# Order of a gated pair's low part and of a weight block's high part in the second expert product

## Chip, cores and metric

The kernel runs on one core of a Trainium2 chip. Its time is the device time of one execution in microseconds; before the change the median of three runs is 1809.54 us (1803.93 to 1812.57). A profile is one further execution, recorded instruction by instruction.

## The reference

One decoder block for 512 tokens of width 1024, all in float32. A normalised input feeds a convolution module and a causal attention with a forgetting gate; both are mixed and added to the input. Then comes a feed-forward part with 16384 single-neuron experts, of which each token takes 128 (8 heads, 16 each, from a product-key search):

```
experts = (e1 * 128 + e2)              # 128 experts for each token
a   = gelu(u[experts] . h) * gates     # peer_u rows, one number per expert
out = sum over experts of a * v[expert] # peer_v rows
x   = x + out;  result = rmsnorm(x)
```

## The kernel before

The first 128 tokens (tile 0) are computed as the reference writes it: GpSimd gathers one row of `peer_u` or `peer_v` per expert slot with an indirect DMA (`fetch`, L1089), and VectorE takes a dot product with it (L1110) or adds it, scaled, to the output (L1116). There are 256 such rows, 128 of each kind, in a generator (`gathered`, L1101) that the main loops call a few rows at a time.

For the other 384 tokens the kernel computes all experts densely. The first expert product multiplies all of `peer_u`, in 128 blocks of 128 experts, with the tokens; its results after gelu are kept in `Sd` in memory, two blocks (a pair) at a time. A gate table `Gd` holds, for every expert and token, the gate or zero. The second expert product, where the change is, multiplies the results by the gates and by `peer_v`: for each of 128 blocks, a weight of 128 experts x 1024 and the gated values of 128 experts x 384 tokens, accumulated over all blocks in six PSUM tiles (L1261 to L1276).

TensorE works in a float32 format of reduced width, so every operand X is split into a high part (rounded copy, made by ScalarE) and a low part (X minus the high part, made by VectorE), and each product is three matmuls (`mm3`, L170): low of the left with high of the right, high with low, high with high. The left operand is the gated pair, `ah` and `al`; the right is the weight block, `whi` and `wlo`. A block has 3 token tiles x 2 column halves x 3 = 18 matmuls, in the order `al`x`whi` (L172), `ah`x`wlo` (L173), `ah`x`whi` (L174).

Weights come through a stream. SP's queue loads raw blocks `wraw` (three buffers), a split gives `whi` and `wlo` (four buffers of each). `next_w` (L162) hands block i to the product and calls `pump` (L135). `pump` first calls `flush` (L122), which issues the splits that are pending: `whi` on ScalarE, `wlo` on VectorE. Then it issues the next raw load, and then it only notes block i+3 as pending. So in block i's call the split of block i+2 is issued, high and low together.

`a_pair` (L1182) prepares the next pair at the start of every second block: it issues on ScalarE's queue the loads of a later `Sb` (L1179) and, every fourth pair, of a later `G` (L1171); VectorE multiplies `Sb` by `G` (L1192); then `split` (L205) issues `ah` on ScalarE (L206) and `al` on VectorE (L208), which needs `ah`. There are two buffers of `ah` and of `al`. The order in which the code issues instructions is the order on each engine; nothing reorders them.

VectorE's order in an even block is thus: the product `Sb`, `al`, one `wlo`, one or two gathered rows; in an odd block: one `wlo`, one or two rows.

Of the kernel before, what the change touches and what calls it, by code (L numbers as in the profile page):

```python
# [9 lines left out]
F32 = mybir.dt.float32  # L10
# [5 lines left out]
AF = mybir.ActivationFunctionType  # L16
ALU = mybir.AluOpType
# [70 lines left out]
def body(ctx, tc, x, xT, w_ct, w_v, w_f, w_co, w_fo, w_o, w_q, keys, pu, pv, pur, vecs, conv_w,  # L88
         bf, g2, gf, maskneg, sel, out):
    nc = tc.nc  # L90
    pool = nc.gpsimd
    dve = nc.vector
# [29 lines left out]
    def flush(hi_to=4, lo_to=4):  # L122
        q = D // 4
        for p in pend:
            eng, lo, raw, hi, nh, nl = p
            if nh < hi_to:
                nc.scalar.activation(hi[:, nh * q:hi_to * q], raw[:, nh * q:hi_to * q], AF.Copy)  # L127
                p[4] = hi_to
            if nl < lo_to:
                c = slice(nl * q, lo_to * q)  # L130
                eng.tensor_tensor(lo[:, c], raw[:, c], hi[:, c].bitcast(F32), op=ALU.subtract)  # L131
                p[5] = lo_to
        pend[:] = [p for p in pend if p[5] < 4]

    def pump(n_split, n_raw):  # L135
        flush()
        while state["raw"] < min(n_raw, len(stream)):
            i = state["raw"]
            raws[i] = base.tile([P, D], F32, tag="wraw", name="wraw", bufs=WRAW)
            if i:  # L140
                nc.sync.dma_start(raws[i], stream[i][0])
            else:
                for c in (slice(0, 512), slice(512, D)):
                    nc.sync.dma_start(raws[i][:, c], stream[i][0][:, c])
                    nc.sync.dma_start(xTt[:, c.start // 512, :], xT[c.start // 512])
            state["raw"] += 1
        while state["split"] < min(n_split, len(stream)):
            i = state["split"]
            kind = stream[i][2]
            if kind != "w":  # L150
                if kind not in dest:
                    return
                hi, lo = dest[kind].pop(0)
            else:
                hi = base.tile([P, D], F32R, tag="whi", name="whi", bufs=WSPL)
                lo = base.tile([P, D], F32R, tag="wlo", name="wlo", bufs=WSPL)
            raw = raws.pop(i)
            pend.append([stream[i][1], lo, raw, hi, 0, 0])
            parts[i] = (hi, lo)
            state["split"] += 1  # L160

    def next_w(held=0):  # L162
        i = state["used"]
        state["used"] += 1
        pump(i + WSPL - held, i + WSPL - held + WRAW - 1)
        if any(p[1] is parts[i][1] for p in pend):
            flush()
        return parts.pop(i)

    def mm3(o, l, r, first, last):  # L170
        (lh, ll), (rh, rl) = l, r
        nc.tensor.matmul(o, ll, rh, start=first, stop=False)  # L172
        nc.tensor.matmul(o, lh, rl, start=False, stop=False)  # L173
        nc.tensor.matmul(o, lh, rh, start=False, stop=last)  # L174
# [30 lines left out]
    def split(hi, lo, src, scale=None):  # L205
        nc.scalar.activation(hi, src, AF.Copy, scale=1.0 if scale is None else scale)  # L206
        if scale is None:
            dve.tensor_tensor(lo, src, hi.bitcast(F32), op=ALU.subtract)  # L208
        else:
            dve.scalar_tensor_tensor(lo, src, scale, hi.bitcast(F32), op0=ALU.mult, op1=ALU.subtract)  # L210
# [920 lines left out]
    def bgrun(us, g):  # L1131
        debt[g] = debt.get(g, 0.0) + us
        while debt[g] > 0:
            r = next(g, None)
            if r is None:
                return False
            debt[g] -= r[0]
        return True
# [3 lines left out]
    def u_block(b):  # L1142
        c, n = divmod(b, SB2)
        kept = c >= NK // SB2 - KEEP
        if n == 0:
            if kept:
                gel[c] = vp[0].tile([P, SB2, TD], F32, tag="kept", name="kept", bufs=KEEP)
            else:
                gel[c] = gl.tile([P, SB2, TD], F32, tag="gel", name="gel", bufs=2)
        p = proj(hden, False)  # L1150
        nc.scalar.activation(gel[c][:, n, :], p[:, :TD], AF.Gelu_apprx_tanh)  # L1151
        if n == SB2 - 1:
            if kept:
                Ss[c] = gel.pop(c)
            else:
                nc.sync.dma_start(Sd[c], gel.pop(c))
# [9 lines left out]
    def load_g(n):  # L1166
        if n >= NK // GB8:
            return
        g = VORD[n * GB8] // GB8
        t = vp[0].tile([P, TD // TG, GB8, TG], F32, tag="G", name="G", bufs=GLD)  # L1170
        nc.scalar.dma_start(t.rearrange("p g b t -> p g (b t)"), Gd[g])  # L1171
        Gs[g] = t

    def load_s(n):
        if n >= NK // SB2 or n < KEEP:
            return
        c = VORD[n * SB2] // SB2
        t = vp[0].tile([P, SB2, TD], F32, tag="S", name="Sb", bufs=3)
        nc.scalar.dma_start(t, Sd[c])  # L1179
        Ss[c] = t  # L1180

    def a_pair(k):  # L1182
        if k >= NK // SB2:
            return
        c = VORD[k * SB2] // SB2
        g, n = divmod(c * SB2, GB8)
        if n == 0:
            load_g(k * SB2 // GB8 + GLD - 1)
        load_s(k + 2)
        a = Ss.pop(c)  # L1190
        a4 = a.rearrange("p n (g t) -> p n g t", t=TG)
        dve.tensor_tensor(a4, a4, Gs[g][:, :, n:n + SB2, :].rearrange("p g n t -> p n g t"), op=ALU.mult)  # L1192
        hi = vp[0].tile([P, SB2, TD], F32R, tag="ah", name="ah", bufs=ABUF)
        lo = vp[0].tile([P, SB2, TD], F32R, tag="al", name="al", bufs=ABUF)
        split(hi, lo, a)
        As[k] = (hi, lo)

    def open_second():
        while bgrun(12, bgr) or later:
            while later:  # L1200
                later.pop(0)()
        gp_ctx.close()
        pd_ctx.close()
        vp.append(ctx.enter_context(tc.tile_pool(name="phe", bufs=1, side="right")))
# [3 lines left out]
    for b in range(UE + 1, NK):  # L1208
        u_block(b)
        room = U_DVE  # L1210
        if len(later) > busy:
            later.pop(0)()
            room += U_SC
        share = U_BG if ready else 0.0
        busy = bgrun(room - share, bgr)
        more = busy or later
        if ready:
            bgrun(share if more else U_END, bgg)
        if not vp and (not more or b == NK - VAHEAD):
            open_second()  # L1220
            opened = b
        if vp and b == min(opened + VWAIT, NK - KEEP * SB2 + 1):
            vready.append(1)
            for g in range(GLD - 1):
                load_g(g)
        if b == NK - KEEP * SB2 + 4:
            a_pair(0)
    gl_ctx.close()
    h2_ctx.close()

# [30 lines left out]
    for b in range(NK - SB2):  # L1261
        c, n = divmod(b, SB2)
        if n == 0:
            a_pair(c + 1)
        hi, lo = next_w()
        ah, al = As[c]
        if b == 0:
            left = 2 * NG - ngath[0]
        while 2 * NG - ngath[0] > left * (NK - 5 - b) // (NK - 4):
            if next(bgg, None) is None:  # L1270
                break
        for i in range(1, NT):
            k = slice((i - 1) * P, i * P)
            for f, d in enumerate(halves):
                mm3(oacc[i - 1][f], (ah[:, n, k], al[:, n, k]), (hi[:, d], lo[:, d]), b == 0, False)
# [89 lines left out]
```

## Time and profile before

| What | Value |
|---|---|
| Profiled execution, own time | 1810.52 us |
| Its span, first to last instruction | 1808.5 us |
| Mean granted TensorE clock | 0.997 of full speed |
| VectorE (DVE) busy | 1507.4 us |
| ScalarE (ACT) busy | 877.3 us |
| GpSimd (POOL) busy | 388.0 us |
| Bytes moved | 432.92 MB, 239 GB/s |
| Landing of a load of `Sb` / `G`, median | 6.6 us / 10.0 us |

PE is TensorE's matmuls, PEld its weight loads, SPq and ACTq DMA issues. Engines overlap, so busy times don't add up. A matmul's recorded duration includes its pipeline, so consecutive ones overlap; the distance between two starts is the pace. In the profile the second expert product is the stretch from about 1257 to 1799 us, with PE lines named `whi,al`, `wlo,ah` and `whi,ah`.

### The profile page before, as it was taken

The page shows a single profiled execution, that of the slowest core. Times are in us where ns is not written, and L with a number is a line of the kernel's source. Part 1 is how long each engine was busy: PE and PEld are TensorE (multiplying, and loading weights), DVE is VectorE, ACT ScalarE, POOL GpSimd, SP SyncE. Part 2 cuts the span into 40 slices and gives each one's busy share as a digit, 9 for nine tenths or more (in the row PEclk, how much of TensorE's full clock was granted, in tenths as well). Part 3 has the DMA queues.
Part 4 walks back from the last instruction along what each step waited for, and adds up shares of the span by engine and source line. Part 5 has one row for each costly group of instructions (what it writes and reads, how often), then busy time and mean ns, then how long its engine had stood idle before and what let it go on. Part 6 is the DMA issues. An engine that isn't in the chain of part 4 may idle for free.

```text
span 1808.5 us, 25395 instructions
## 1 busy us (share of the span) xinstructions
PE 1767.8 (98%) x9289; PEld 1538.4 (85%) x9289; DVE 1507.4 (83%) x2649; ACT 877.3 (49%) x1622; POOL 388.0 (21%) x303
## 2 busy tenths in 40 slices
PE   8999999999999999999999999999999999999997
PEld 7887777788888889999999999999787787787786
DVE  5799999998755699999888987766888888888887
ACT  5665665535524323344488499953333333333333
POOL 0000000000000000023322322143443444454440
PEclk9999999999999999999999999999999999999999
DMA  6332222122343125578989899999999999999994
GB/s 224 97 94 72 86 76 80 61 82 93 117 148 129 63 78 161 180 250 286 312 277 319 313 314 320 318 355 408 369 384 382 372 385 380 378 384 373 373 335 147
DMA packets 164477, 432.92 MB, mean 239 GB/s; under 512 B 13696, under 2 KB 63488, under 8 KB 162304
## 3 DMA queue, kind: packets, MB, share of 16 engines
q1 hardware_dynamic: 111840, 239.37, 38.5%
q0 software_dynamic: 39424, 138.43, 21.6%
q10 hardware_dynamic: 13088, 53.50, 7.8%
q8 instruction: 73, 1.20, 0.3%
q14 instruction: 52, 0.43, 0.1%
HBM read 376.20 MB, written 50.86 MB: 236 GB/s over the span
## 4 chain that ended last, share of the span: by engine, by line
PE 50%; DVE 22%; ACT 12%; DMA 10%; issue 5%; ACTq 0%; POOL 0%; SPq 0%; POOLq 0%; DVEq 0%
PE mm L172 15%; PE mm L173 15%; PE mm L174 15%; DMA wraw<-in_pv 7%; DVE wlo L131 5%; DVE x L1116 5%; DVE y L498 5%; ACT whi L127 4%; ACT ohs L1067 2%; DMA wraw<-in_pu 2%; ACT ah L206 2%; DVE Sb L1192 2%; PE pvp L1076 2%; DVE grow L1110 2%; DVE ptl L637 1%
## 5 line engine op out<-in xcount | busy, mean ns | idle before, releaser
L131 DVE TENSOR_TENSOR wlo<-wraw,whi 128x1024 fp32r<-128x1024 f32 (+1 forms) x434 | 432.8, 1005 | 101.3 <-ACT whi L127 97.1
L127 ACT ACTIVATE whi<-wraw 128x1024 fp32r<-128x1024 f32 (+1 forms) x429 | 373.7, 893 | 94.6 <-DMA wraw<-in_pv 38.8
L172 PE MATMUL mm<-h2h,wlo 128*128 128x384 f32 (+1 forms) x1152 | 397.8, 345 | 2.1 <-DVE wlo L131 1.6
L173 PE MATMUL mm<-h2l,whi 128*128 128x384 f32 (+1 forms) x1152 | 392.8, 341 | 0.5 <-DVE h2l L208 0.5
L174 PE MATMUL mm<-h2h,whi 128*128 128x384 f32 (+1 forms) x1152 | 393.0, 341 | 0.0
L1097 POOL DMA_INDIRECT grow<-in_pur,sx x128 | 179.1, 1399 | 613.8 <-DVE grow L1110 369.1
L1097 POOL DMA_INDIRECT grow<-in_pv,sx x128 | 185.9, 1452 | 230.1 <-DVE x L1116 203.4
L172 PEld LDWEIGHTS mm<-h2h,wlo 128*128 128x128 f32 x1152 | 216.8, 188 | 7.6 <-DVE wlo L131 2.0
L173 PEld LDWEIGHTS mm<-h2l,whi 128*128 128x128 f32 x1152 | 217.1, 188 | 5.7 <-DVE h2l L208 1.1
L174 PEld LDWEIGHTS mm<-h2h,whi 128*128 128x128 f32 x1152 | 216.8, 188 | 5.3
L173 PE MATMUL mm<-wlo,ah 128*128 128x512 f32 x512 | 203.4, 397 | 9.4 <-DVE wlo L131 9.0
L172 PE MATMUL mm<-whi,al 128*128 128x512 f32 x512 | 199.9, 390 | 0.2 <-DVE al L208 0.2
L174 PE MATMUL mm<-whi,ah 128*128 128x512 f32 x512 | 199.7, 390 | 0.0
L206 ACT ACTIVATE ah<-Sb 128x768 fp32r<-128x768 f32 x60 | 50.8, 846 | 303.9 <-DVE Sb L1192 254.5
L498 DVE SCALAR_TENSOR_TENSOR y<-z,cw,y 128x512 f32<-128x512 f32 x240 | 174.2, 749 | 1.1 <-ACT y L495 0.2
L1116 DVE SCALAR_TENSOR_TENSOR x<-grow,dots,x 128x1024 f32<-128x1024 f32 x128 | 164.5, 1285 | 1.1
L172 PE MATMUL mm<-hTh,wlo 128*128 128x512 f32 x384 | 161.3, 420 | 3.2 <-DVE qa L570 1.7
L1110 DVE SCALAR_TENSOR_TENSOR grow<-grow,hd 128x1024 f32<-128x1024 f32 x128 | 155.0, 1217 | 0.7 <-DMA grow<-in_pur,sx 0.7
L174 PE MATMUL mm<-hTh,whi 128*128 128x512 f32 x384 | 150.6, 392 | 0.0
L173 PE MATMUL mm<-hTl,whi 128*128 128x512 f32 x384 | 150.0, 391 | 0.0
L1151 ACT ACTIVATE gel<-mm 128x384 f32<-128x384 f32 x118 | 57.7, 489 | 182.4 <-PE mm L174 110.1
L173 PEld LDWEIGHTS mm<-wlo,ah 128*128 128x128 f32 x512 | 96.0, 188 | 41.9 <-DVE wlo L131 23.0
(284 smaller groups left out, 2943.9 us busy)
## 6 DMA issues: line engine op xcount, KB each, us to landing
wraw<-in_pu SPq DMA_DIRECT2D x128, 512.0 KB, 4.9
wraw<-in_pv SPq DMA_DIRECT2D x128, 512.0 KB, 6.4
wraw<-in_w_ct SPq DMA_DIRECT2D x48, 512.0 KB, 3.5
Gd<-gst SPq DMA_DIRECT2D x24, 1024.0 KB, 9.8
G<-Gd ACTq DMA_DIRECT2D x16, 1536.0 KB, 10.0
Sb<-Sd ACTq DMA_DIRECT2D x60, 384.0 KB, 6.6
Sd<-gel SPq DMA_DIRECT2D x59, 384.0 KB, 6.1
wraw<-in_w_q SPq DMA_DIRECT2D x16, 512.0 KB, 3.5
```

Source lines behind the costliest of these rows:

```text
L127: nc.scalar.activation(hi[:, nh * q:hi_to * q], raw[:, nh * q:hi_to * q], AF.Copy)
L131: eng.tensor_tensor(lo[:, c], raw[:, c], hi[:, c].bitcast(F32), op=ALU.subtract)
L172: nc.tensor.matmul(o, ll, rh, start=first, stop=False)
L173: nc.tensor.matmul(o, lh, rl, start=False, stop=False)
L174: nc.tensor.matmul(o, lh, rh, start=False, stop=last)
L206: nc.scalar.activation(hi, src, AF.Copy, scale=1.0 if scale is None else scale)
L498: dve.scalar_tensor_tensor(acc, z[:, w:w + S], cw[:, j, w:w + 1], acc, op0=ALU.mult, op1=ALU.add)
L1067: nc.scalar.activation(o[:, 3, g, :, t], o[:, 1, g, :, t], AF.Copy, scale=gl32[:, t0 + u:t0 + u + 1])
L1097: pool.indirect_dma_start(out=t, out_offset=None, in_=src, in_offset=bass.IndirectOffsetOnAxis(ap=sx[:, n % NG:n % NG + 1], axis=0))
L1110: yield 1.25, dve.scalar_tensor_tensor(t, t, 1.0, hd, op0=ALU.mult, op1=ALU.mult, accum_out=dots[:, k:k + 1])
L1116: yield 1.28, dve.scalar_tensor_tensor(o, t, dots[:, k:k + 1], o, op0=ALU.mult, op1=ALU.add)
L1151: nc.scalar.activation(gel[c][:, n, :], p[:, :TD], AF.Gelu_apprx_tanh)
```

## The change

`a_pair` no longer issues `al` itself. It issues `ah` and puts the subtraction on a list `apend`; `a_low` issues what is on the list. In the first product's loop (first pair) `a_low` follows `a_pair` at once; in the second product it is called behind the block's gathered rows. And each block of the second product calls `flush(4, 0)` behind `next_w`: it issues the whole high part of whatever is pending (block i+3) and none of its low part, which stays pending until the next block's `flush`.

```
         hi = vp[0].tile([P, SB2, TD], F32R, tag="ah", name="ah", bufs=ABUF)
         lo = vp[0].tile([P, SB2, TD], F32R, tag="al", name="al", bufs=ABUF)
-        split(hi, lo, a)
+        nc.scalar.activation(hi, a, AF.Copy)
         As[k] = (hi, lo)
+        apend.append(lambda: dve.tensor_tensor(lo, a, hi.bitcast(F32), op=ALU.subtract))
+
+    apend = []
+
+    def a_low():
+        while apend:
+            apend.pop(0)()
...
         if b == NK - KEEP * SB2 + 4:
             a_pair(0)
+            a_low()
...
         if n == 0:
             a_pair(c + 1)
         hi, lo = next_w()
+        flush(4, 0)
         ah, al = As[c]
         if b == 0:
             left = 2 * NG - ngath[0]
         while 2 * NG - ngath[0] > left * (NK - 5 - b) // (NK - 4):
             if next(bgg, None) is None:
                 break
+        a_low()
         for i in range(1, NT):
```

## Rows read from the trace of the kernel before

**Rows 1.** The page, part 1: busy us, share of the span, instructions.
```profile
PE 1767.8 (98%) x9289; PEld 1538.4 (85%) x9289; DVE 1507.4 (83%) x2649; ACT 877.3 (49%) x1622; POOL 388.0 (21%) x303
```

**Rows 2.** The page, part 4: chain that ended last, shares by engine.
```profile
PE 50%; DVE 22%; ACT 12%; DMA 10%; issue 5%; ACTq 0%; POOL 0%; SPq 0%; POOLq 0%; DVEq 0%
```

**Rows 3.** Second product: us, PE, PEld, DVE, ACT, POOL busy, clock, DMA share, GB/s.
```profile
1257.00:1799.00 542.00, 532.41 (x2306) 429.20 (x2304) 468.82 (x469) 180.82 (x204) 230.66 (x161) 1.00 0.95 359
```

**Rows 4.** Waits, 1257 to 1799 us: us in total, times, longest us.
```profile
DVE al L208 <- ACT ah L206: 61.1, 63, 1.2
...
ACT whi L127 <- DMA wraw<-in_pv: 35.9, 17, 4.3
...
PEld mm L173 <- DVE wlo L131: 23.0, 40, 1.0
...
DVE wlo L131 <- ACT whi L127: 8.3, 9, 1.8
```

**Rows 5.** Timeline of VectorE, two pairs: start us, us, instruction [idle before <-releaser].
```profile
1434.05 0.96 DVE L208 TENSOR_TENSOR al<-Sb,ah 128x768 fp32r<-128x768 f32 x1 [1.24 <-ACT ah L206]
...
1441.58 0.96 DVE L208 TENSOR_TENSOR al<-Sb,ah 128x768 fp32r<-128x768 f32 x1 [0.96 <-ACT ah L206]
1442.53 1.23 DVE L131 TENSOR_TENSOR wlo<-wraw,whi 128x1024 fp32r<-128x1024 f32 x1
1443.67 2.60 DVE L1116 SCALAR_TENSOR_TENSOR x<-grow,dots,x 128x1024 f32<-128x1024 f32 x2
...
1448.57 0.95 DVE L1192 TENSOR_TENSOR Sb<-Sb,G 128x768 f32<-128x768 f32 x1
1450.47 0.96 DVE L208 TENSOR_TENSOR al<-Sb,ah 128x768 fp32r<-128x768 f32 x1 [0.96 <-ACT ah L206]
```

**Rows 6.** Timeline of TensorE: first and last start, two blocks, first and last stalls.
```profile
1257.05 0.39 PE L172 MATMUL mm<-whi,al 128*128 128x512 f32 x1
...
1273.84 0.50 PE L173 MATMUL mm<-wlo,ah 128*128 128x512 f32 x1
...
1405.01 0.39 PE L172 MATMUL mm<-whi,al 128*128 128x512 f32 x1
...
1409.09 0.39 PE L172 MATMUL mm<-whi,al 128*128 128x512 f32 x1
...
1409.89 0.50 PE L173 MATMUL mm<-wlo,ah 128*128 128x512 f32 x1 [0.42 <-DVE wlo L131]
...
1766.70 0.39 PE L174 MATMUL mm<-whi,ah 128*128 128x512 f32 x1
...
1798.74 0.39 PE L174 MATMUL tp<-whi,ah 128*128 128x512 f32 x1
```

**Rows 7.** Timelines of VectorE and TensorE at the start of the second product.
```profile
1261.07 0.96 DVE L1192 TENSOR_TENSOR kept<-kept,G 128x768 f32<-128x768 f32 x1
...
1263.94 1.22 DVE L131 TENSOR_TENSOR wlo<-wraw,whi 128x1024 fp32r<-128x1024 f32 x1
...
1265.26 0.39 PE L172 MATMUL mm<-whi,al 128*128 128x512 f32 x1
...
1267.38 1.22 DVE L131 TENSOR_TENSOR wlo<-wraw,whi 128x1024 fp32r<-128x1024 f32 x1
```

**Rows 8.** Raw blocks: landing in the stretch; a late load and its two `wlo`.
```profile
DMA to landing us min/median/max: 3.4/6.3/11.3
...
1281.17 1.23 DVE L131 TENSOR_TENSOR wlo<-wraw,whi 128x1024 fp32r<-128x1024 f32 x1
...
1282.42 10.44 DMA wraw<-in_pv
...
1294.04 1.22 DVE L131 TENSOR_TENSOR wlo<-wraw,whi 128x1024 fp32r<-128x1024 f32 x1 [1.83 <-ACT whi L127]
```

**Rows 9.** DMA totals: first 1300 to 1700 us, then 1220.7 to 1266.
```profile
DMA packets 39654, 151.05 MB, mean 378 GB/s; under 512 B 4396, under 2 KB 4396, under 8 KB 38097
...
DMA packets 4481, 18.51 MB, mean 409 GB/s; under 512 B 509, under 2 KB 509, under 8 KB 4175
```

More of the change, by code (lines that the diff above doesn't have):

```diff
@@ L1194, in a_pair, with a_low @@
         lo = vp[0].tile([P, SB2, TD], F32R, tag="al", name="al", bufs=ABUF)
-        split(hi, lo, a)
+        nc.scalar.activation(hi, a, AF.Copy)
         As[k] = (hi, lo)
+        apend.append(lambda: dve.tensor_tensor(lo, a, hi.bitcast(F32), op=ALU.subtract))
+    apend = []
+    def a_low():
+        while apend:
+            apend.pop(0)()
     def open_second():
@@ L1227, in body @@
             a_pair(0)
+            a_low()
     gl_ctx.close()
@@ L1265, in body @@
         hi, lo = next_w()
+        flush(4, 0)
         ah, al = As[c]
@@ L1271, in body @@
                 break
+        a_low()
         for i in range(1, NT):
```

## Prediction

> **What bounds the kernel now.** I read the page's busy times first: TensorE is busy for 98% of the span [rows 1], which by itself leaves nothing to gain. The chain of waits tells otherwise: half of it is TensorE and 22% VectorE [rows 2]. The change touches only the second expert product, so everything below is read in its stretch, 1257 to 1799 us, where VectorE is busy for 468.8 of 542 us [rows 3].
>
> The waits of that stretch [rows 4] name who holds whom. VectorE waits 61.1 us, 63 times, for ScalarE's `ah` before it can form `al`, and 8.3 us for `whi`. TensorE's weight loader waits for `wlo` 40 times. VectorE's busy time and its two waits add up to 538.2 of 542 us: it has no free time in the stretch, though it is busy for only 86% of it.
>
> The timeline shows how. A pair of blocks with three gathered rows takes VectorE 8.89 us from one `al` to the next (1441.58 to 1450.47), a pair with two takes 7.53 us (1434.05 to 1441.58); in both, 0.96 us pass idle between the end of the `Sb` product and `al`, which is ScalarE making `ah` [rows 5]. TensorE needs 4.08 us for an undisturbed block (1405.01 to 1409.09), so 8.16 for a pair [rows 6]. So VectorE falls behind by 0.73 us in a three-row pair and gains 0.63 in a two-row one. The price is in [rows 6]: at 1409.89 a matmul on `wlo` starts 0.80 us after the one before it, where the pace is 4.08/18 = 0.227, because that `wlo` had just been finished.
>
> I went through the starts of all 2304 matmuls of the stretch. A step that is more than 0.1 us over the pace occurs 55 times, first at 1273.84 and last at 1766.70 (a late `wlo` also stretches the step behind it) [rows 6]; the excess sums to 17.2 us. Checked from outside: first start 1257.05, last 1798.74, so about 541.9 us for 128 blocks; 128 x 4.08 = 522.2. Of the 19.7 us between, 17.2 are these stalls and 2.5 are small irregularities that the change does not address. 17.2 us is what there is to win; the 61 us of `al` waits is not, since TensorE becomes the bound long before.
>
> **The change part by part.** No instruction is added or removed: the same `ah`, `al`, `whi`, `wlo`, and the same transfers on SP, ScalarE and GpSimd queues. Two orders change.
>
> First, `al`. It moves from directly behind ScalarE's `ah` to behind the next `wlo` and the block's gathered rows. The 0.96 us in which `ah` is made is now covered by that `wlo`, whose successor starts 1.14 us later (1442.53 to 1443.67), and by at least one row of 1.28 us [rows 5]. That takes 0.96 us out of VectorE's pair: 8.89 becomes 7.93 and 7.53 becomes 6.57, against 8.16 of TensorE. So even the three-row pair now gains 0.23 us of lead on TensorE, the other 1.59. VectorE's total need falls to 468.8 + 8.3 = 477 us, below 522: the bound moves to TensorE. If that cover were gone (the `wlo` not ready to run), the wait only moves, and nothing is saved.
>
> Second, the high part `whi` of the newest weight block. It is issued at the end of a block's `next_w`, no longer at the start of the following one: 125 of 128 `whi`, all behind `ah` on ScalarE. This is what makes the first part work: the next block's `wlo` now finds `whi` done, where it used to stand behind `ah` on ScalarE. ScalarE is busy for 181 of 542 us [rows 3], so its time is free. The cost: a ScalarE that waits for a transfer now does so in front of `ah` and of the loads of `Sb` and `G`, which sit on its queue. The longest such wait is 4.3 us, the mean 35.9/17 = 2.1 [rows 4]. A load of `Sb` is for two pairs later, 16 us, so it can bear this; a late `ah` is borne by `al`, which has a `wlo` and the rows ahead of it. Bounds from these rows: 0, or 17 waits x up to 4.3 = 73 us of ScalarE if each came through, which it can't as long as VectorE has a lead. I take 0. Nothing below 0 beyond the stalls already counted. The SP queue keeps its order, and its raw load still waits for the `wlo` that frees the buffer.
>
> What the delay of `al` costs. TensorE's first matmul of a pair is the one on `al`; it used to be the `wlo` behind it that came last. VectorE has no lead at the start: `wlo` for block 2 starts at 1263.94, 1.3 us before block 2 does (1265.26). After the change VectorE goes from the first product (1261.07 + 0.96 = 1262.03) into `wlo` and two rows, 3.44 us as in 1263.94 to 1267.38, so `al` starts at 1265.47 and ends at 1266.43 [rows 7]. TensorE waits 1.2 us for it, once; from then on the lead grows. Bounds: 0, and 2.4 if it happens twice before the lead is there. I take 1.2.
>
> What is late next: transfers. In the stretch VectorE waits for `whi` 9 times, 8.3 us together, where a raw block came late [rows 4]. Landing takes 6.3 us in the median and 11.3 at most [rows 8]. Three blocks of TensorE are 12.24 us, and a chain of load, `whi`, `wlo` over three buffers took 12.86 us in its late case (`wlo` 1281.17 + 1.23, load 10.44, `whi`, `wlo` 1294.04 + 1.22) [rows 8]: 0.6 us late, which a lead of one or two pairs covers. Bounds: 0 if the lead takes all, 8.3 if every wait comes through to TensorE. I take 1.0, near the lower end, since the four hidden split buffers let VectorE lead by up to two blocks.
>
> The sum: 17.2 - 1.2 - 1.0 = 15.0 us. The profiled execution took 1810.5 us (span 1808.5 and 2.0 around it), so 1795.5. The median of the runs is 1.0 lower, 1809.5, so 1794.5; I say 1795.
>
> **The rivals.**
> *Late transfers keep their price.* If the lead does not build, the 8.3 us of `whi` waits all become TensorE stalls: 17.2 - 1.2 - 8.3 = 7.7, giving 1802. For it: the chain of waits has transfers of about 10 us at intervals, as the 10.44 one [rows 8]. Against: VectorE gains 0.23 to 1.59 us in every pair.
>
> *The transfers bind.* From 1300 to 1700 us the queues moved 151.05 MB, 378 GB/s [rows 9]. Without the stalls there (12.8 of the 17.2 by the same walk) they must move it in 387 us, 390 GB/s. If 378 is all they give, only the 4.4 us outside remain, less 1.2: 3.2, giving 1806. Against it: 409 GB/s over the 45 us from 1221 [rows 9], and only 8.3 us of VectorE waits on late blocks. The Trainium skill's "DMA: Bandwidth & Descriptors" (section "Where 436 GB/s comes from") speaks for this rival: traffic between HBM and SBUF is held to about 358 GB/s, one core's share of its memory. By that rule the stretch's mean of 359 GB/s [rows 3] would be the bound itself and the change worth nothing, 1809.5. The trace disagrees, with 378 and 409 GB/s; the skill's "HBM Reference" ("Specifications (TRN2)") gives the reason, that the share counts when both cores of a pair stream, and one core runs here.
>
> *It does not do what it says.* `wlo` behind the `Sb` product waits for a `whi` that is not done, as long as `al` waited. VectorE's need stays, the 1.2 us come on top: 1811. Against: `whi` has a whole block, 4 us, for some 1.2 us of work (load landed 1282.42 + 10.44 = 1292.86, `wlo` released 1294.04 [rows 8]).
>
> *Slower: the ring of three raw blocks.* A `wlo` frees the buffer, the load lands L later, `whi` and `wlo` follow: (L + 2.4)/3 us for a block. Today's block is 541.9/128 = 4.23 us, which the ring exceeds from L = 10.3 on. VectorE no longer pauses, so loads, rows and `Sb` come closer together; if that drives a normal landing from 6.3 to the 10.44 of the late case, 128 x 4.29 = 549 us, 7 more than today, with 1.2 on top: 1818. For it: a landing of 11.3 occurs already. Against: the median is 4.0 us below the point.
>
> **How the numbers follow.** Forecast 0.68, late transfers 0.12, transfers bind 0.09, no effect 0.04, slower 0.07. About 0.5%, 9 us, is what a measurement of this kernel can tell from no change. Nearly all of the forecast and a third of the late-transfer case lie below 1800.5, so faster 0.70; the rest of them, the binding transfers and no effect make 0.24; slower 0.06. The range goes from 1789 (all 19.7 us gone, 1789.8) to 1807, which takes in the first two rivals with their terms and leaves the last two out.
>
> **What would show it.** Right: `al` waits for `ah` near 0; TensorE's waits for `wlo` down to a few; the 128 blocks within about 527 us; VectorE idle for some 50 us in the stretch, now waiting for `whi` or `ah` held by TensorE's buffers; a single wait of TensorE on `al` near the start. Wrong: `wlo` waits for `whi` about as long as `al` did; repeated waits of TensorE on `al`; raw blocks landing at 10 us in the median; blocks still at 4.2 us with VectorE waiting on transfers.

## The result and the profile after

The changed kernel takes 1794.57 us (median of five runs, 1790.93 to 1798.04) against 1809.54 us before: a ratio of 0.9916, 95% interval 0.9899 to 0.9933, 15.0 us less where 15 were forecast. The profiled execution took 1790.9 us, near the low end of the scatter, so its own gain of 19.6 us is above the median's.

Nearly all of it, 18.9 of the 19.6 us of the profiles, is in the second product. Its 2304 matmuls started over 541.7 us before [rows 6] and over 522.8 us now. This is the stretch in the changed kernel, with the columns of [rows 3]:

```profile
1256.60:1779.70 523.10, 522.64 (x2306) 432.28 (x2304) 466.76 (x465) 185.38 (x203) 233.33 (x159) 1.00 0.95 371
```

TensorE is busy for all of it. VectorE does the same work (466.8 us busy, 468.8 before) within a stretch that is 19 us shorter. First start, one stall and last start on TensorE:

```profile
1256.64 0.39 PE L172 MATMUL mm<-whi,al 128*128 128x512 f32 x1
...
1264.62 0.39 PE L174 MATMUL tp<-whi,ah 128*128 128x512 f32 x1
1265.46 0.47 PE L172 MATMUL mm<-whi,al 128*128 128x512 f32 x1 [0.46 <-DVE al L1197]
...
1779.41 0.39 PE L174 MATMUL tp<-whi,ah 128*128 128x512 f32 x1
```

From 1264.62 to 1265.46 is a step of 0.84 us between two starts, 0.61 over the pace of 0.227. It is the only step of the stretch that is more than 0.1 us late, where there were 55. The waits of the same stretch (us in total, times, longest us) answer to [rows 4]:

```profile
ACT ah L1195 <- PE tp L174: 158.2, 54, 3.0
ACT whi L127 <- PE tp L174: 104.8, 46, 2.3
ACT whi L127 <- DMA wraw<-in_pv: 51.9, 20, 7.4
...
DVE al L1197 <- ACT ah L1195: 31.9, 34, 2.6
DVE wlo L131 <- ACT whi L127: 10.5, 9, 3.9
...
PE mm L172 <- DVE al L1197: 0.5, 1, 0.5
```

The direction of waiting is reversed. ScalarE now waits 263 us for TensorE to give back the buffers of `ah` and `whi`, and VectorE waits behind it: the makers are ahead of the consumer and stopped by its buffers. VectorE still waits 31.9 us for `ah`, but TensorE waits for `al` once. The chain that ended last was half TensorE before [rows 2]; now it is by engine:

```profile
PE 79%; DVE 10%; ACT 6%; DMA 3%; issue 1%; POOL 0%; SPq 0%; POOLq 0%; ACTq 0%; DVEq 0%
```

### The profile page after: what moved, and what is told of

The parts are those of the page before. It is cut to its first block, busy times and chain, and to the rows that moved or that the text cites. A ratio compares the mean times of both kernels' runs of the same rounds, so it can differ in the third digit from the quotient of the medians.

```text
span 1789.2 us, 25445 instructions
## 1 busy us (share of the span) xinstructions
PE 1758.5 (98%) x9289; PEld 1541.9 (86%) x9289; DVE 1507.7 (84%) x2649; ACT 882.5 (49%) x1622; POOL 394.4 (22%) x303
## 4 chain that ended last, share of the span: by engine, by line
PE 79%; DVE 10%; ACT 6%; DMA 3%; issue 1%; POOL 0%; SPq 0%; POOLq 0%; ACTq 0%; DVEq 0%
PE mm L172 22%; PE mm L173 21%; PE mm L174 21%; DVE y L498 4%; PE tp L173 3%; PE tp L174 3%; PE tp L172 3%; ACT ohs L1067 3%; DVE wlo L131 2%; PE pvp L1076 2%; DMA wraw<-in_pu 1%; ACT whi L127 1%; DVE ptl L637 1%; DVE mx L608 1%; ACT Pt L618 1%
## 5 line engine op out<-in xcount | busy, mean ns | idle before, releaser
L127 ACT ACTIVATE whi<-wraw 128x1024 fp32r<-128x1024 f32 (+1 forms) x429 | 378.6, 894 | 218.1 <-PE tp L174 104.8
L173 PE MATMUL mm<-wlo,ah 128*128 128x512 f32 x512 | 199.3, 389 | 0.0
L1067 ACT ACTIVATE ohs<-ohs,gl 128x128 f16<-128x128 f16 x384 | 118.3, 438 | 7.8 <-DVE ohs L1062 7.8
```

The source lines that it names most:

```text
L1067: nc.scalar.activation(o[:, 3, g, :, t], o[:, 1, g, :, t], AF.Copy, scale=gl32[:, t0 + u:t0 + u + 1])
```

## The experiments

Theory: VectorE's occupancy bound the second product; taking ScalarE's time for `ah` out of VectorE's order hands the bound to TensorE. Rivals: the sooner `whi` gains by hiding late transfers; the transfers bind; only the moved `al` matters.

Times are medians (of 4 to 10 runs; two runs for two raw buffers); the ratio is to the kernel before, run beside each, with medians of 1807.2 to 1809.5 us. "Stretch" is first to last matmul start of the second product in one profile; "late steps" is the time over the pace, in us, of its steps that are more than 0.1 us late. The profiled execution is one run and can lie well off the median.

| Kernel | us | Ratio, 95% interval | Stretch | Late steps |
|---|---|---|---|---|
| before | 1809.5 | | 541.7 | 17.2 |
| changed | 1794.6 | 0.9916 (0.9899 to 0.9933) | 522.8 | 0.6 |
| changed, again | 1794.4 | 0.9922 (0.9904 to 0.9941) | 524.7 | 2.5 |
| low part alone | 1854.4 | 1.026 (1.0237 to 1.0282) | 585.0 | 55.9 |
| high part alone | 1810.4 | 1.0009 (0.9996 to 1.0023) | 533.6 | 8.8 |
| low part behind the weight | 1790.2 | 0.9902 (0.9884 to 0.9919) | 522.1 | 0 |
| VectorE product of 384 | 1793.7 | 0.9923 (0.9902 to 0.9945) | 524.1 | 1.9 |
| VectorE product of 1024 | 1811.3 | 1.0013 (1.0001 to 1.0024) | 541.0 | 17.0 |
| 256 KB more | 1818.3 | 1.0055 (1.0037 to 1.0073) | 546.8 | 23.6 |
| 512 KB more | 1847.3 | 1.0215 (1.0193 to 1.0238) | 579.2 | 55.3 |
| 256 KB on ScalarE's queue | 1812.2 | 1.0016 (1.0003 to 1.0029) | 546.3 | 23.3 |
| two raw buffers | 1896.7 | 1.0489 (1.0452 to 1.0527) | 603.9 | 79.7 |
| first high part sooner | 1792.0 | 0.9909 (0.9894 to 0.9923) | 523.8 | 1.7 |
| both, low part behind the weight | 1791.1 | 0.9915 (0.9899 to 0.9931) | 522.1 | 0 |

**The changed kernel again.**

> The changed kernel once more, for a second profile and for a yardstick beside the next three. Theory (TensorE bounds the second product at 4.08 us a block once VectorE has a lead): its 128 blocks take 522 to 524 us, with no stall after the first pair, whatever the whole time; 1794 +/- 4 us. Rival (the profiled execution was a lucky one, and in the median one transfers still hold blocks back): a stretch of some 526 us, the 4 us by which the median lies above the profiled execution.

The stretch is 524.7 us, with one late step of 2.5 us in the first pair and none after. Theory held. Something else scatters too: over the profiles with three raw buffers the second product starts between 1254.1 and 1261.3 us, though everything up to its first pair is the same code.

**Each part alone.**

```
 # low part alone: the changed kernel without
-        flush(4, 0)
 # high part alone: the kernel before, with
         hi, lo = next_w()
+        flush(4, 0)
```

> Only the low part of the pair is moved; the weight's high part stays at the start of the next block, so behind the pair's high part on ScalarE. Theory (the two parts work only together): VectorE's next split waits 0.85 + 1.05 us behind the Sb product instead of 0.96, 1.9 us a pair; pairs of 7.93 + 1.9 and 6.57 + 1.9 us, 9.3 in the mean against TensorE's 8.16, so the stretch is about 590 us and the kernel 1855 to 1865 us, slower than before. Rival (moving the low part is what gains, the high part is an extra): 1795 to 1800 us.

1854 us, just under the range expected and 46 us slower than before. VectorE in that kernel (columns as in [rows 5]):

```profile
1440.79 0.95 DVE L1192 TENSOR_TENSOR Sb<-Sb,G 128x768 f32<-128x768 f32 x1
1443.65 1.23 DVE L131 TENSOR_TENSOR wlo<-wraw,whi 128x1024 fp32r<-128x1024 f32 x1 [1.91 <-ACT whi L127]
...
1449.19 0.95 DVE L1192 TENSOR_TENSOR Sb<-Sb,G 128x768 f32<-128x768 f32 x1
1452.05 1.23 DVE L131 TENSOR_TENSOR wlo<-wraw,whi 128x1024 fp32r<-128x1024 f32 x1 [1.91 <-ACT whi L127]
```

The wait has doubled, since `wlo` now needs a `whi` that stands behind `ah`. The pair from 1443.65 to 1452.05 has two gathered rows and takes 8.40 us. Moving `al` alone is a loss.

> Only the weight's high part is issued a block sooner; the pair's low part stays directly behind its high part. Theory: VectorE still waits 0.96 us a pair, so it stays the bound: stretch 540 us, 1807 to 1811 us. Rival (the sooner high part takes late transfers out of VectorE's way, which gains by itself): the 8.3 us of waits for it go, 1801 us or less.

The median of ten runs is level with before, so the sooner `whi` doesn't make the gain by itself, and the rival's 1801 us are excluded. Two waits of its profile, 1261.3 to 1795 us, and the longest of the first:

```profile
DVE al L208 <- ACT ah L206: 65.6, 63, 2.4
...
DVE wlo L131 <- ACT whi L127: 3.1, 3, 1.3
```

```profile
1397.32 1.06 ACT L127 ACTIVATE whi<-wraw 128x1024 fp32r<-128x1024 f32 x1 [6.14 <-DMA wraw<-in_pv]
1398.29 0.83 ACT L206 ACTIVATE ah<-Sb 128x768 fp32r<-128x768 f32 x1
```

Against [rows 4] VectorE's waits for a late `whi` fell by 5.2 us, but its waits for `ah` rose by 4.5: a `whi` that waits for its raw block now stands ahead of `ah`. The 533.6 us of the stretch mislead, because TensorE began the second product at 1261.3 us, later than in any other profile with three raw buffers; it ended at 1794.9, against 1798.7 before. VectorE's own way from the first to the last product of this loop with `G` took 518.1 us (1262.80 to 1780.94) against 523.9 before (1261.07 to 1784.94). So this execution, the second fastest of its ten (1806.4 us), did save VectorE some 6 us; the median doesn't show them, and that is left open.

**How much room VectorE has.** A product whose result nothing reads, once a pair:

```
         a_low()
+        if n == 0:
+            junk = sb.tile([P, 384], F32, tag="xw", name="xw", bufs=1)   # or 1024
+            dve.tensor_tensor(junk, gfb[:, :384], gfb[:, :384], op=ALU.mult)
```

> The changed kernel with one idle VectorE product more in every pair (128 x 384, an estimated 0.56 us), its result unused. Theory (VectorE needs 477 us of 523 and has 46 to spare): 63 x 0.56 = 35 us fit, stretch 523 us, kernel unchanged at 1795 us. Rival (VectorE's occupancy is what counts, each us saved or spent shows): a good part of 35 us comes back, 1810 us or more.

> The same with a product of 128 x 1024, 1.22 us. Theory: 477 + 63 x 1.22 = 554 us, over TensorE's 522: VectorE is the bound again, stretch about 554 us, kernel 1822 to 1830 us. Rival (the gain came from the high part's earlier start or from transfers, not from VectorE's time): well under that, 1800 us.

The small one is free and the large one gives the whole gain back, as the theory has it, but at 1811 us where it had 1822 to 1830. Its timeline tells why:

```profile
1442.00 0.95 DVE L1192 TENSOR_TENSOR Sb<-Sb,G 128x768 f32<-128x768 f32 x1
1442.87 1.21 DVE L131 TENSOR_TENSOR wlo<-wraw,whi 128x1024 fp32r<-128x1024 f32 x1
1444.01 2.59 DVE L1116 SCALAR_TENSOR_TENSOR x<-grow,dots,x 128x1024 f32<-128x1024 f32 x2
1446.52 0.95 DVE L1197 TENSOR_TENSOR al<-Sb,ah 128x768 fp32r<-128x768 f32 x1
1447.39 1.22 DVE L1285 TENSOR_TENSOR xw<-gfb 128x1024 f32<-128x1024 f32 x1
1448.52 1.22 DVE L131 TENSOR_TENSOR wlo<-wraw,whi 128x1024 fp32r<-128x1024 f32 x1
...
1450.85 0.95 DVE L1192 TENSOR_TENSOR Sb<-Sb,G 128x768 f32<-128x768 f32 x1
```

Consecutive instructions overlap: the added one lasts 1.22 us but takes 1.13 from its start to the next (1447.39 to 1448.52), and `al`, which lasts 0.95, takes 0.87. The pair with three rows is 8.85 us (1442.00 to 1450.85), so 8.85 - 1.13 = 7.72 without the added product, where the prediction had 7.93. The old pair of 8.89 us was thus 1.17 us longer, and not 0.96. Three lines of the kernel before tell why:

```profile
1440.70 0.85 ACT L206 ACTIVATE ah<-Sb 128x768 fp32r<-128x768 f32 x1 [4.79 <-DVE Sb L1192]
1441.46 1.04 ACT L127 ACTIVATE whi<-wraw 128x1024 fp32r<-128x1024 f32 x1
...
1447.33 1.32 DVE L1116 SCALAR_TENSOR_TENSOR x<-grow,dots,x 128x1024 f32<-128x1024 f32 x1
```

Besides the 0.96 us idle, the overlap of `al` with the `Sb` product was lost, 0.08 us. Then `wlo` started at 1442.53, 0.95 us after `al` and just behind the end of its own `whi` (1441.46 + 1.04 = 1442.50), which stood behind `ah` on ScalarE: another 0.08. The last 0.05 is a gathered row of 1.32 us, 1.28 here, and has nothing to do with the wait. In the kernel with the high part alone `al` waits as long, but `whi` is done, and `wlo` follows after 0.88 us:

```profile
1441.44 0.96 DVE L208 TENSOR_TENSOR al<-Sb,ah 128x768 fp32r<-128x768 f32 x1 [0.96 <-ACT ah L206]
1442.32 1.22 DVE L131 TENSOR_TENSOR wlo<-wraw,whi 128x1024 fp32r<-128x1024 f32 x1
```

The old order thus cost 1.12 us a pair, and the product of 1.13 put in its place restores the old time within 3 us.

**How near the transfers are.**

```
         a_low()
+        if n == 0:
+            junk = sb.tile([P, 512], F32, tag="xw", name="xw", bufs=2)   # or 1024
+            nc.sync.dma_start(junk, pu[b][:, :512])                      # or nc.scalar
```

> The changed kernel with a load of 256 KB more in every pair on SP's queue, into a tile that nothing reads: 63 x 0.262 = 16.5 MB on 194 MB. Theory (transfers are not the bound up to at least the 409 GB/s seen): 211 MB in 523 us are 403 GB/s, stretch 523 to 527 us, kernel 1795 to 1799 us. Rival (the transfers bind at about the 371 GB/s that the stretch now has): 211/0.371 = 568 us, kernel 1840 us.

> The same with 512 KB in every pair, 33 MB on 194. Theory: 227 MB in 523 us would be 434 GB/s, more than any stretch has shown; at 409 GB/s it takes 555 us, so the transfers are the bound here, stretch about 555 us, kernel about 1827 us, with raw blocks landing at 9 us or more. Rival (transfers have room well beyond this): 1797 us. Rival (they bind at 371): 612 us, kernel 1884 us.

> As the kernel with 256 KB more in every pair (1818 us), the added load on ScalarE's queue instead of SP's. Theory (bytes bind: it ran at 403 GB/s between 1300 and 1700 us and the one with 512 KB at 406): the same cost, 1813 to 1823 us, again some 403 GB/s. Rival (the added load stands ahead of raw blocks on SP's queue and lets them land later, bytes have room): 1795 to 1800 us and over 410 GB/s.

The first two cost some 20 us more than the theory had; the third came out as its theory said, within a us. 256 KB a pair cost 24 us on SP's queue and 18 on ScalarE's. I had spread the bytes over the whole stretch; between 1300 and 1700 us the changed kernel already moves more than its mean. DMA totals of that window, first the changed kernel, then the three:

```profile
DMA packets 41911, 158.84 MB, mean 397 GB/s; under 512 B 4659, under 2 KB 4659, under 8 KB 40352
```

```profile
DMA packets 46058, 161.24 MB, mean 403 GB/s; under 512 B 5134, under 2 KB 5134, under 8 KB 44602
```

```profile
DMA packets 42930, 162.40 MB, mean 406 GB/s; under 512 B 4770, under 2 KB 4770, under 8 KB 41502
```

```profile
DMA packets 46488, 163.19 MB, mean 408 GB/s; under 512 B 5165, under 2 KB 5165, under 8 KB 44969
```

At TensorE's pace the first two would need 429 and 461 GB/s (397, and 0.262 or 0.524 MB every 8.16 us); 403 to 408 are given, however much is asked. So the rival that 378 binds is refuted (397 is moved with no stall), but a bound lies 1.5 to 3% above. Most of it is the bytes: on the other queue 18 of the 24 us stay. The other 6 go with the queue, as the two ratios' intervals don't overlap. That the stretches are alike (546.3 against 546.8) says little, as the profile on SP's queue was the fastest of its five runs (1812.4 us) and the one on ScalarE's the slowest of its ten (1815.8). What moves is who waits: with SP's queue the raw blocks are late, with ScalarE's the gathered rows. First a line of the former, then two of the latter:

```profile
DVE wlo L131 <- ACT whi L127: 69.6, 49, 4.5
```

```profile
DVE x L1116 <- DMA grow<-in_pv,sx: 44.5, 34, 4.0
...
DVE wlo L131 <- ACT whi L127: 17.4, 13, 3.2
```

The Trainium skill's "DMA: Bandwidth & Descriptors" ("Where 436 GB/s comes from") holds such traffic to about 358 GB/s. This trace disagrees, with 397 to 408 GB/s on one core.

**The ring of raw buffers.** `WRAW = 3` becomes `WRAW = 2`.

> The changed kernel with two raw weight buffers instead of three, in the whole kernel. Theory (a block can't be faster than (L + 2.4)/buffers, L the landing of a raw block): with L = 6.5 to 7.7 us a block of 4.5 to 5.0 us, so the second product takes 570 to 640 us instead of 523, TensorE waiting for the splits; the first product suffers too, the kernel is over 1880 us. Rival (landing is shorter when fewer loads are under way, so two buffers do): L falls under 5.8 and the stretch stays within 530 us.

A stretch of 603.9 us, 4.72 a block, inside the theory's range. But the formula is only a floor: with the measured median landing of 6.2 us it gives (6.2 + 2.4)/2 = 4.3. The rest may be the unevenness of landings (3.5 to 10.6 us), which two buffers smooth less than three; no run separates that. The granted clock was 0.97 in this stretch with its long pauses, 1.00 in the changed kernel's; how much of the time that took is not separated either.

**The first pair.** The low part directly behind the weight's (`a_low()` moved to just behind `flush(4, 0)`); the first high part sooner (one `flush(4, 0)` ahead of the loop); and both.

> As the changed kernel, but the pair's low part stands directly behind the next weight's low part and ahead of the gathered rows. Theory: one split of 1.14 us covers the 0.96 us of the pair's high part, so the stretch is the same 523 us, without the 0.6 us stall at the first pair; 1794 us. Rival (the gathered rows are needed as cover, since the high part waits for TensorE's buffers): VectorE's waits for the high part come back in every pair and with them stalls of TensorE, 1800 us or more.

> The changed kernel with the high part of block 2 issued once before the loop, so that the first pair's high part is not ahead of it on ScalarE. In four profiles of the changed order VectorE waited 1.92 us for it and TensorE then 0.6 to 3.3 us for the first pair's low part. Theory: the 1.92 us go, TensorE's one stall shrinks to 0 to 1.4 us; 1792 to 1794 us. Rival (the stall is a late transfer): 1.92 us stay.

> The low part directly behind the weight's low part (1790 us) and the first high part before the loop. Theory: no stall was left in the former, so this one is the same: stretch 522 us, 1788 to 1793 us, about 4 us below the changed kernel. Rival (the 4 us were scatter between executions): 1794 us.

With `al` ahead of the gathered rows no late step is left in either profile (522.1 us; 128 x 4.08 = 522.2): one weight split covers ScalarE's `ah`, and the rows are not needed. With only the first `whi` issued before the loop, VectorE's 1.92 us wait in front of block 2's `wlo` is gone and the late step is 1.6 us; that execution entered the second product with VectorE behind for another reason, as its previous `wlo` had waited 2.3 us. These versions' medians are 1790.2, 1792.0 and 1791.1 against 1794.4 and 1794.6, but the ratios' intervals overlap, so I can show the missing stall and not a gain of 4 us. Directly behind the weight is the best order found: its ratio, 0.9902, is the lowest, though not apart from the others'.

## Why the prediction was right, step by step

*VectorE sets the pace, TensorE takes over.* Shown from both sides: the stalls are gone, a VectorE product of 0.55 us is free, one of 1.22 us restores the old time. The prediction's argument for it, busy time and waits that fill the stretch, was not enough by itself: in the changed kernel VectorE's 466.8 us and its waits (53 us) fill 520 of 523 us too, and TensorE is the bound. What tells them apart is who ends the waits, ScalarE's work on VectorE's own product before, TensorE's buffers now.

*15.0 us.* The mechanism is right; that the medians agree to the tenth is luck. By its profile the gain in the stretch is 17.2 + 2.3 - 0.6 = 18.9 us, by the second one 17.2 + 2.3 - 2.5 = 17.0. The terms below err in both directions, and the interval of the median's gain is 12 to 18 us.

*17.2 us of stalls.* Right: 55 late steps became one. The 2.5 us of "small irregularities that the change does not address" nearly all went too: 124 of the 127 distances from block to block are 4.08 us now, 82 before. So most were also VectorE's lateness, in steps under 0.1 us.

*1.2 us for the delayed `al`.* Right in kind and place, off in size. In the seven profiles with three raw buffers that have `al` behind the rows and `whi` ahead of the next pair, without the extra flush, TensorE stalls for `al` at block 2, by 0.6, 2.5, 1.9, 3.2, 3.3, 3.0 and 3.2 us. The prediction counted 125 of 128 `whi` as moved, but overlooked that `wlo` for block 2 needs one of the other three, noted before the loop, which stands behind `ah` on ScalarE. In the changed kernel's profile:

```profile
1258.06 0.95 DVE L1192 TENSOR_TENSOR kept<-kept,G 128x768 f32<-128x768 f32 x1
1260.93 1.23 DVE L131 TENSOR_TENSOR wlo<-wraw,whi 128x1024 fp32r<-128x1024 f32 x1 [1.92 <-ACT whi L127]
```

*1.0 us for late transfers.* Measured 0. VectorE still waits 10.5 us for `whi`, none of which reaches TensorE: the lead covers it.

*7.93 us, 477 us.* VectorE's need was mis-sized: 7.72 for a three-row pair. The prediction took out the idle 0.96 us alone and read the pair of 8.89 as if its other steps stayed; with the wait go two overlaps of 0.08 us that it had cost, and 0.05 was a slow row. The sum did not depend on it, as either is below 8.16.

*What would show it.* I said waits for `ah` near 0 and, a line on, VectorE idle and held by TensorE's buffers. The second came (31.9 us for `ah`, held by TensorE); the first contradicts it. An idle VectorE behind a full buffer costs nothing.

*The rivals.* No effect: a `wlo` that waits for `whi` is what the low part alone shows, and its wait is 1.91 us, not the 0.96 I priced it at: it costs 46 us where I had 1. Transfers bind: 378 was wrong, 403 to 408 is right, so it was closer than I thought. The ring: with three buffers it did not bind the changed kernel. Landing rose from 6.3 to 7.4 us in the median (changed kernel again), short of the 10.3 that the rival needed.

Left open: why the profiles scatter by some 7 us in the start of the second product, why the high part alone saves VectorE time in its profile but none in the median, and whether the best order is faster than the changed kernel by more than its first stall.

## What to carry to other kernels

Where an engine is not fully busy, add its waits to its busy time over the stretch: if the sum fills it, ask who ends the waits. Where it is another engine's work on this engine's own product, the engine is the bound, and a wait inside its order costs as much as work; where it is a buffer that the consumer gives back, the consumer is the bound. Fill such a wait with independent work of the same engine, but first see that this work's own input is not queued behind the very instruction that is waited for: either half of this change alone gained nothing or lost 46 us. The gain ends at the next bound, so read the price from the consumer's stalls (17 us) and not from the wait that goes (61 us).

## What the runs showed of the hardware

VectorE instructions that wait for nothing overlap by 0.08 us or a little more: 128x768 lasts 0.95 us and takes 0.87 from start to start, 128x1024 lasts 1.22 and takes 1.13. One that waits loses this overlap with the instruction before it but keeps it with the one behind, if that one has its inputs (0.88 us from `al` to `wlo` in the kernel with the high part alone). And on this one core, transfers of rows, weight blocks and gate tables together reach 403 to 408 GB/s over 400 us and no more in the three kernels that ask for more, while the changed kernel's mix at 397 leaves no stall.
